# Attention outputs divided and gated as they leave PSUM, with the order of work drawn anew

## The chip, the cores and the metric

The kernel runs on one core of a Trainium2 chip. The core has five engines with instruction queues of their own: TensorE (PE in the profile; PEld is its weight load), VectorE (DVE), ScalarE (ACT), GpSimd (POOL) and SyncE (SP), which here issues all DMAs. Each queue is worked off in its order; engines wait for each other through semaphores. SBUF is the on-chip memory, PSUM the accumulator memory that TensorE writes. The metric is device time in microseconds (us) from start to end of one execution.

## The reference

Two layers are applied to x (1024 tokens x 1024 channels). Shortened, with shapes left out:

```
h = rms_norm(x, pre_norm);  proj = h @ w_in        # split into q, k, v and gates of three branches
oa = softmax(q1 k1) v - lam * softmax(q2 k2) v     # 6 differential heads, two softmaxes each
oa = rms_norm(oa, diff_subln) * (1 - lambda_init) * silu(dgate)
ob = softmax(q k) v * silu(ggate)                  # 6 grouped-query heads, 2 key heads
om = softmax(mq mk) mv * silu(mgate)               # 4 heads over 256 memory tokens
y = concat(oa, ob, om) @ w_out;  x = x + rms_norm(y, post_norm)
```

## The kernel before, in words

A planner in Python decides the order of everything. Each piece of work is a generator that asks for an engine (with an assumed duration and a priority), a buffer or a PSUM bank; an event loop (`Plan`) keeps an assumed clock and writes the instructions down in the order in which it starts them. On the chip only that order stands: the assumed durations (`ACT`, `DVE`, `LAT`, `DVE_FIX`, `SLACK`) and figures such as `DU` (spacing of score units) or `GS_ORDER` (order of heads) have no other effect.

A layer has three stretches. First come the projections: token tiles of 128 rows times column chunks of 256 (L520; 24 products to a chunk and tile, since each fp32 product is made as hi x hi + hi x lo + lo x hi). The first five chunks go ahead (`FIRST`); nine more (`REST`) are worked off beside the differential heads. What leaves PSUM is rotated (L661, L663), split, transposed (L707) and stored to DRAM; gate columns become (1 + tanh(g/2)) * g (L728, L736) and go to the scratch tensor `g_scr`.

Second, attention. There are 12 score items of the differential heads (two to a head), then 6 grouped (`g`) and 4 memory (`m`) heads in the order of `GS_ORDER`. An item has a pass for row maxima (L1071; L1283/L1284; L1338/L1339: a product of 512 columns, then a maximum on DVE, L942), a transposition of the negated maxima (L917), and units of 1024 scores per query block (L1081; L1295/L1296; L1349/L1350), each followed by exp on ACT (L898), an fp16 copy (L902, mostly ACT) and an fp16 remainder (L905, mostly POOL; L904 on DVE). Probabilities times values (PV, L531 to L533) take a bank called `pv`; V has a column of ones, so column 64 of the result is the row sum.

What happens to a PV result is what the change touches. Before, ACT copies 65 columns per query tile into an SBUF tile `o` (L994) and frees the bank. After a head's last PV, its closing steps run on whole heads of 512 columns: `fin_d` (L1161) for a differential head, `fin_g` (L1196) for the others; the gate comes by DMA into a tile `gt` (`gate_in`, L1108), the output goes to a tile `yst` and by DMA to `y_scr`.

Third, the output projection (L1448), normalisation and residual; the first tile's products fill the end of the attention.

PSUM: four single banks `ps` shared by the kinds of `KINDS` (third number 1), two double ones `pp`. In `KINDS` the second number is how many banks a kind may hold: `mx` (maxima) 4 before.

Of the kernel before, what the change touches and what calls it, by code (L numbers as in the profile page):

```python
# [22 lines left out]
P = 128  # L23
# [35 lines left out]
E_BUFS, E_MORE, O_BUFS = 4, 2, 3  # L59
# [9 lines left out]
DU = (3.0, 0.0)  # L69
# [3 lines left out]
GS_ORDER = ('g0', 'm0', 'g1', 'm1', 'g2', 'm2', 'g3', 'm3', 'g4', 'g5')  # L73
LAT = {"pe": 0.231, "act": 0.176, "dve": 0.165, "pool": 0.121, "hwdge": 0.65, "dma": 0.95}
DVE_FIX = 0.15
# [5 lines left out]
SLACK = 0.8  # L81

KINDS = {'un': (0.5, 2, 2), 'z': (1, 2, 2), 's0': (2, 2, 1), 's1': (0, 2, 1), 'st': (1, 4, 1), 'pv': (1, 1, 1), 'tr': (-1, 2, 1), 'mx': (2, 4, 1), 'zh': (3, 2, 1)}
# [204 lines left out]
def trunk(ctx, tc, t_in, t_out):  # L288
# [42 lines left out]
    def ACT(n, fn, prio=0, src="s"):  # L331
        return use("act", (0.2 if src == "s" else 0.17) + n / 1200.0, fn, prio)
# [31 lines left out]
    g_scr = dram.tile([P, 16, NT, HD], F32, name="g_scr")  # L364
# [53 lines left out]
    def vscale(vmax, gmx, w, sc, key):  # L418
# [20 lines left out]
        yield DVE(4, f, ops=4)  # L439
# [9 lines left out]
    def rstd_of(ss, n, inv, box, prio=0):  # L449
# [3 lines left out]
        def f():  # L453
            pool.tensor_scalar(out=u[:, :n], in0=ss, scalar1=inv, scalar2=EPS, op0=ALU.mult, op1=ALU.add)  # L454
            pool.tensor_tensor(out=r[:, :n], in0=u[:, :n], in1=mhalf[:, :n], op=ALU.pow)  # L455
# [83 lines left out]
    def make_layer(l):  # L539
# [185 lines left out]
        def put_gate(ps, t, c, freed):  # L725
# [156 lines left out]
        o_d, o_g, yst = {}, {}, {}  # L882

        def open_attn():
# [8 lines left out]
            R["o"] = Bag([at.tile([P, NT, 66], F32, name=f"o{i}") for i in range(O_BUFS)])  # L893
# [81 lines left out]
        def pv_part(it, u, es, evs, prev, mine):  # L975
# [7 lines left out]
            if it.new_o(u):  # L983
                yield from it.alloc_o()
# [8 lines left out]
            v = ps[:, 0:66 * n].rearrange("p (i d) -> p i d", d=66)  # L993
            yield ACT(65 * n, lambda: act.activation(it.o_dst(u), v[:, :, 0:65], AF.Copy), SV_PRIO, "p")  # L994
# [55 lines left out]
        def mk_d(m, prev):  # L1050
# [38 lines left out]
            it.new_o = lambda u: u == 1 and m % 2 == 0  # L1089

            def alloc_o():
                o_d[h] = []
                for _ in range(2):
                    o_d[h].append((yield take("o")))

            it.alloc_o = alloc_o
            it.o_dst = lambda u: o_d[h][m % 2][:, u - 1:u + 1, 0:65]
# [10 lines left out]
        def gate_in(hd):  # L1108
            c = {0: "dg0", 1: "dg0", 2: "dg0", 3: "dg0", 4: "dg1", 5: "dg1", 12: "dg1", 13: "dg1",
                 10: "gg1", 11: "gg1", 14: "gg1", 15: "gg1"}.get(hd, "gg0")  # L1110
            yield wait(gate_ev[c])
            i = yield take("gt")
            g = Q["v"].tile([P, NT, HD], F32, name="gt", bufs=2)
            yield wait(dmas([(g, g_scr[:, hd], 256)]))
            return g, i

        def y_tile(hd):
            if hd % 2 == 0:
                yst[hd // 2] = yield take("yst")
            return yst[hd // 2][:, :, hd % 2, :]  # L1120

        def y_done(hd):
            if hd % 2 == 1:
                kt = hd // 2
                c = kt * P
                t = yst.pop(kt)
# [34 lines left out]
        def fin_d(h, gate):  # L1161
            o = o_d.pop(h)
            cv = sc["d0" if h < 4 else "d1"]
            r = small.tile([P, 2, 8], F32, name="rz")
            if h in (0, 4):
                def f():
                    pool.tensor_scalar(out=cv[:, 2:3], in0=cv[:, 1:2], scalar1=2.0, scalar2=0.0,
                                       op0=ALU.mult, op1=ALU.add)
                    pool.tensor_tensor(out=cv[:, 3:4], in0=cv[:, 2:3], in1=sc["lam"], op=ALU.mult)

                yield POOL(1, f, FIN, ops=4)
            yield DVE(130, lambda: [dve.reciprocal(out=r[:, i], in_=o[i][:, :, 64]) for i in range(2)], FIN, ops=2)
            fi = yield take("ft")
            t = [Q["sd"].tile([P, NT, HD], F32, name="ft", bufs=2) for _ in range(2)]
            for i in range(2):
                yield DVE(512, lambda: dve.scalar_tensor_tensor(
                    out=t[i], in0=o[i][:, :, 0:64], scalar=cv[:, 2 + i:3 + i], in1=bc(r[:, i]),
                    op0=ALU.mult, op1=ALU.mult), FIN, port=True)
                free("o", o[i])
            yield DVE(512, lambda: dve.tensor_sub(out=t[0], in0=t[0], in1=t[1]), FIN, port=True)  # L1180
            yield ACT(512, lambda: act.activation(t[1], t[0], AF.Square), FIN)
            ss = small.tile([P, 8], F32, name="ss8")
            yield DVE(512, lambda: dve.tensor_reduce(out=ss, in_=t[1], axis=AX.X, op=ALU.add), FIN)
            box = []
            yield from rstd_of(ss, 8, 1.0 / HD, box, FIN)
            g, gi = gate
            yield DVE(512, lambda: dve.tensor_mul(out=t[0], in0=t[0], in1=g), FIN, port=True)
            free("gt", gi)
            ys = yield from y_tile(h)
            yield DVE(512, lambda: dve.tensor_tensor(out=ys, in0=t[0], in1=bc(box[0][:, :8]), op=ALU.mult), FIN,  # L1190
                      port=True)
            free("ft", fi)
            yield from y_done(h)

        def fin_g(hd, cv, gate):
            g, gi = gate  # L1196
            o = o_g.pop(hd)
# [701 lines left out]
```

## Time and profile before

| | us |
|---|---|
| runs | 1515.41, 1521.71, 1523.19 (median 1521.71) |
| the profiled execution | 1515.87 |
| its span, first to last instruction | 1514.1 |
[...]
| DVE / ACT / POOL busy | 1012.3 / 893.3 / 909.2 |

The page's busy times are unions of an engine's instructions; PE's idle time is the difference to the span. The view of stages (windows) gives the same by stretch. The view of waits says who ended an idle stretch, and the timeline the order of single instructions with the idle time before them in brackets.

### The profile page before, as it was taken

The numbers are of one execution on the slowest core, as the hardware profiler recorded it, in microseconds if no ns is written. First come the engines' busy times: TensorE is split into PE (matmuls) and PEld (weight loads), VectorE is DVE, ScalarE is ACT, GpSimd is POOL, SyncE is SP. The second block draws the span as 40 slices with busy tenths as digits, with TensorE's granted clock in tenths as the row PEclk, the third lists the DMA queues.
The fourth block names the chain that finished last, engine by engine and source line by source line (L and its number), as shares of the span: only waits on it lengthen the run. The fifth ranks groups of instructions, "written<-read, shape, count | busy, mean of one in ns | idle before, by whom it ended". The sixth has DMA issues, their size and how long they took to land.

```text
span 1514.1 us, 39223 instructions
## 1 busy us (share of the span) xinstructions
PE 1469.9 (97%) x15920; PEld 1362.8 (90%) x15920; DVE 1012.3 (67%) x1887; ACT 893.3 (59%) x1429; POOL 909.2 (60%) x653
## 2 busy tenths in 40 slices
PE   8999999999999999999999999999999999999997
PEld 7999989999999988888899989999999998788886
DVE  6738686777773897825466486776777649876233
ACT  5333747776677587663333346677667757686511
POOL 4233848889777586661132358579888757685400
PEclk9999999999999999999999999999999999999999
DMA  6544313233223644116164524223341256322232
GB/s 220 158 121 130 86 59 107 81 109 106 78 65 93 187 120 105 49 50 214 70 213 129 141 70 117 70 63 101 111 113 58 64 136 195 94 68 72 98 136 98
DMA packets 166658, 164.75 MB, mean 109 GB/s; under 512 B 14924, under 2 KB 140588, under 8 KB 166477
## 3 DMA queue, kind: packets, MB, share of 16 engines
q1 hardware_dynamic: 166477, 162.25, 36.7%
q8 instruction: 125, 2.05, 0.5%
q14 instruction: 56, 0.46, 0.1%
HBM read 111.74 MB, written 50.09 MB: 107 GB/s over the span
## 4 chain that ended last, share of the span: by engine, by line
PE 84%; DVE 5%; issue 3%; POOL 3%; DMA 2%; ACT 1%; SPq 1%; POOLq 0%; DVEq 0%; ACTq 0%
PE ps L520 35%; PE pp L1448 10%; PE pp L1081 6%; PE ps L1071 6%; PE ps L531 4%; PE ps L533 4%; PE ps L532 4%; PE ps L1283 3%; PE ps L1284 2%; PE pp L1295 2%; PE pp L1296 2%; POOL el L905 2%; PE ps L476 2%; DVE mx L942 1%; PE ps L707 1%
## 5 line engine op out<-in xcount | busy, mean ns | idle before, releaser
L905 POOL TENSOR_TENSOR el<-e,eh 128x1024 f16<-128x1024 f32 x254 | 562.6, 2229 | 167.3 <-ACT eh L902 160.1
L520 PE MATMUL ps<-wt,big 128*128 128x256 f32 x4608 | 642.1, 286 | 12.6 <-DVE sl L716 3.4
L520 PEld LDWEIGHTS ps<-wt,big 128*128 128x128 f32 x4608 | 605.0, 191 | 32.7 <-DVE sl L716 3.9
L942 DVE TENSOR_REDUCE mx<-ps 128x1 f32<-128x512 f32 (+1 forms) x608 | 404.0, 684 | 118.2 <-PE ps L1071 79.4
L898 ACT ACTIVATE e<-pp 128x1024 f32<-128x1024 f32 x304 | 309.2, 1023 | 99.9 <-PE pp L1081 53.8
L902 ACT ACTIVATE eh<-e 128x1024 f16<-128x1024 f32 x264 | 277.6, 1058 | 2.9
L531 PEld LDWEIGHTS <-eh 128*128 128x128 f16 x2144 | 194.4, 96 | 13.6 <-issue 9.0
L533 PEld LDWEIGHTS <-el 128*128 128x128 f16 x2144 | 196.1, 99 | 4.8 <-POOL el L905 4.2
L412 POOL TENSOR_TENSOR wt<-rt,wt 128x512 fp32r<-128x512 f32 x83 | 123.2, 1496 | 126.0 <-ACT wt L410 112.2
L532 PEld LDWEIGHTS <-eh 128*128 128x128 f16 x2144 | 196.2, 97 | 0.9 <-issue 0.8
L1071 PE MATMUL ps<-sdk,sdq 96*128 96x512 f32 x384 | 158.7, 413 | 0.8 <-DVE gs L736 0.8
L454 POOL TENSOR_SCALAR u<-ss 128x1 f32<-128x1 f32 (+3 forms) x95 | 24.2, 254 | 224.6 <-DVE ss L1589 96.1
L531 PE MATMUL ps<-vd,eh 128*128 128x65 f16 x1536 | 150.5, 193 | 0.0
L532 PE MATMUL ps<-vd,eh 128*128 128x64 f16 x1536 | 149.6, 194 | 0.0
L533 PE MATMUL ps<-vd,el 128*128 128x65 f16 x1536 | 149.1, 192 | 0.0
L1081 PE MATMUL pp<-sdq,sdk 98*128 98x256 f32 x768 | 124.9, 285 | 0.2 <-DMA sdq<-nl 0.2
L1081 PEld LDWEIGHTS pp<-sdq,sdk 98*128 98x128 f32 x768 | 113.1, 189 | 5.7 <-issue 0.6
L994 ACT ACTIVATE o<-ps 128x130 f32<-128x130 f32 (+1 forms) x160 | 46.1, 288 | 92.0 <-PE ps L533 91.4
L1295 PE MATMUL pp<-big 128*128 128x256 f32 x384 | 99.2, 290 | 0.0
L1296 PE MATMUL pp<-big 67*128 67x256 f32 x384 | 97.7, 286 | 1.3 <-DMA big<-nl 1.2
L410 ACT ACTIVATE wt<-rt 128x512 fp32r<-128x512 f32 x124 | 75.1, 630 | 18.8 <-DMA rt<-in_w_in 7.1
L455 POOL TENSOR_TENSOR r<-u,mhalf 128x1 f32<-128x1 f32 (+3 forms) x95 | 80.7, 850 | 7.9
(244 smaller groups left out, 2621.9 us busy)
## 6 DMA issues: line engine op xcount, KB each, us to landing
rt<-in_w_in SPq DMA_DIRECT2D x96, 128.0 KB
rt<-in_w_in SPq DMA_DIRECT2D x44, 256.0 KB
gt<-g_scr SPq DMA_DIRECT2D x32, 256.0 KB
rt<-in_w_out SPq DMA_DIRECT2D x32, 256.0 KB
sdq<-s_dqa SPq DMA_DIRECT2D x48, 128.0 KB
sdk<-s_dka SPq DMA_DIRECT2D x48, 128.0 KB
big<-s_gqa SPq DMA_DIRECT2D x24, 256.0 KB
big<-s_gqb SPq DMA_DIRECT2D x24, 256.0 KB
```

What stands on the lines that cost most here:

```text
L520: pe.matmul(ps, lhsT=x[:, kt, :], rhs=y[:, a, :], start=(kt == 0 and n == 0), stop=(kt == KT - 1 and n == 2))
L531: pe.matmul(o[:, 0:65], lhsT=eh, rhs=v[:, kt, 0:65], start=(kt == 0), stop=False, skip_group_check=True)
L532: pe.matmul(o[:, 0:64], lhsT=eh, rhs=v[:, kt, 66:130], start=False, stop=False, skip_group_check=True)
L533: pe.matmul(o[:, 0:65], lhsT=el, rhs=v[:, kt, 0:65], start=False, stop=(kt == n - 1), skip_group_check=True)
L898: yield ACT(1024, lambda: act.activation(e, ps, AF.Exp, scale=scale), 0, "p")
L902: yield either((ACT(1024, lambda: act.activation(eh, e, AF.Copy)), 0.0), (DVE(1024, lambda: dve.tensor_copy(out=eh, in_=e), 0, fast=True, ...
L905: (POOL(1024, lambda: pool.tensor_sub(out=el, in0=e, in1=eh)), 0.0))
L942: yield DVE(512, lambda: dve.tensor_reduce(out=out_ap, in_=src, axis=AX.X, op=ALU.max), MXP[0])
L1071: yield (512, lambda ps, n=n: pe.matmul(ps, lhsT=q()[0:96, i * P:(i + 1) * P], rhs=k()[0:96, n * 512:(n + 1) * 512], start=True, stop=True ...
L1081: pe.matmul(ps[:, a * 256:(a + 1) * 256], lhsT=k()[0:98, kt * P:(kt + 1) * P], rhs=q()[0:98, j * 256:(j + 1) * 256], start=True, stop=True)
L1295: pe.matmul(o, lhsT=ka()[:, ks], rhs=a()[:, qs], start=True, stop=False)
L1448: pe.matmul(z, lhsT=x[:, k, :], rhs=y, start=(k == KT_ORDER[0] and n == 0), stop=(k == KT_ORDER[-1] and n == 2))
```

## The change

- A PV result is divided by its row sum as it leaves PSUM. Even items of a differential head: a reciprocal on DVE, then ACT copies 64 columns per query tile with the reciprocal as scale. Odd items: reciprocal, times lambda, then on DVE one instruction per query tile, PSUM times reciprocal minus the even item's tile (the sign goes into the gain). One `o` tile per head is left instead of two, and `fin_d` shrinks to square, sum, power, two multiplications.
- Grouped and memory heads: reciprocal, times the scale of V, then one DVE instruction per query tile, PSUM times reciprocal times gate, written over the gate. `fin_g` is gone. The gate is loaded straight into the output tile `yst` (two heads in one DMA of 512 KB), before the first PV result of the pair may leave PSUM. `g_scr` is laid out by pairs of heads.
- The sub-norm gain is multiplied into PSUM before the gating instruction instead of after it.
- `GS_ORDER`: grouped heads go two ahead of memory heads. `KINDS`: `mx` holds 3 banks instead of 4. `DU` 3.0 to 3.17, `SLACK` 0.8 to 0.88, assumed costs of ACT and DVE changed.

```diff
-GS_ORDER = ('g0', 'm0', 'g1', 'm1', 'g2', 'm2', 'g3', 'm3', 'g4', 'g5')
+GS_ORDER = ('g0', 'g1', 'm0', 'g2', 'm1', 'g3', 'm2', 'g4', 'm3', 'g5')
-... 'mx': (2, 4, 1) ...
+... 'mx': (2, 3, 1) ...
@@ pv_part
-            yield ACT(65 * n, lambda: act.activation(it.o_dst(u), v[:, :, 0:65], AF.Copy), SV_PRIO, "p")
+            yield from it.evict(it.q0(u), ps[:, 0:66 * n].rearrange("p (i d) -> p i d", d=66), n)
@@ mk_d
+            def evict(q0, v, n):
+                r = small.tile([P, 4], F32, name="rv")
+                if m % 2 == 0:
...
+                    yield DVE(n, lambda: dve.reciprocal(out=r[:, :n], in_=v[:, :, 64]), SV_PRIO)
+                    yield ACT(HD * n, lambda: [act.activation(o[:, q0 + i, :], v[:, i, 0:HD], AF.Copy,
+                                                              scale=r[:, i:i + 1]) for i in range(n)], SV_PRIO, "p", n)
+                else:
...
+                        for i in range(n):
+                            dve.scalar_tensor_tensor(out=o[:, q0 + i, :], in0=v[:, i, 0:HD], scalar=r[:, i:i + 1],
+                                                     in1=o[:, q0 + i, :], op0=ALU.mult, op1=ALU.subtract)
@@ fin_d, the DVE part
-                yield DVE(512, lambda: dve.scalar_tensor_tensor(      # twice
-                    out=t[i], in0=o[i][:, :, 0:64], scalar=cv[:, 2 + i:3 + i], in1=bc(r[:, i]),
-            yield DVE(512, lambda: dve.tensor_sub(out=t[0], in0=t[0], in1=t[1]), FIN, port=True)
-            yield DVE(512, lambda: dve.tensor_mul(out=t[0], in0=t[0], in1=g), FIN, port=True)
-            yield DVE(512, lambda: dve.tensor_tensor(out=ys, in0=t[0], in1=bc(box[0][:, :8]), op=ALU.mult), FIN,
+            yield DVE(512, lambda: dve.tensor_tensor(out=o, in0=o, in1=bc(box[0][:, :8]), op=ALU.mult), FIN, port=True)
+            yield DVE(512, lambda: dve.tensor_mul(out=g, in0=o, in1=g), FIN, port=True)
@@ fin_g becomes gated
-            yield DVE(60, lambda: dve.reciprocal(out=r, in_=o[:, :, 64]), FIN)
-            yield DVE(512, lambda: dve.scalar_tensor_tensor(out=g, in0=g, scalar=cv()[:, 1:2], in1=bc(r),
-            yield DVE(512, lambda: dve.tensor_tensor(out=t, in0=o[:, :, 0:64], in1=g, op=ALU.mult), FIN, port=True)
+                yield wait(has)                                       # the gate has landed
+                    dve.reciprocal(out=r[:, :n], in_=v[:, :, 64])
+                    dve.tensor_scalar(out=r[:, :n], in0=r[:, :n], scalar1=cv()[:, 1:2], scalar2=None, op0=ALU.mult)
+                    for i in range(n):
+                        dve.scalar_tensor_tensor(out=g[:, q0 + i, :], in0=v[:, i, 0:HD], scalar=r[:, i:i + 1],
+                                                 in1=g[:, q0 + i, :], op0=ALU.mult, op1=ALU.mult)
```

How the order moves, at three places. First PE beside the differential heads of layer 0 (`ps_` banks; L520 is L523 after, L707 is L709, L1071 and L1081 are L1070 and L1080). Before:

```order
L1081 MATMUL pp_76<-sdq_1518,sdk_1520 128x256 x4
L520 MATMUL ps_79<-wt,big 128x256 x18
L1081 MATMUL pp_75<-sdq_1518,sdk_1520 128x256 x4
L520 MATMUL ps_79<-wt,big 128x256 x6
L707 MATMUL ps_80<-ident,nat 128x128 x2
L520 MATMUL ps_79<-wt,big 128x256 x6
```

A chunk ends in bank 79 with the fourth row (24 products) and the next chunk starts in the same bank one transposition later. The corresponding stretch after:

```order
L523 MATMUL ps_78<-wt,big 128x256 x6
L709 MATMUL ps_80<-ident,nat 128x128
L1070 MATMUL ps_77<-sdk_1524,sdq_1522 128x512
L523 MATMUL ps_78<-wt,big 128x256 x6
L1070 MATMUL ps_79<-sdk_1524,sdq_1522 128x512
L1080 MATMUL pp_75<-sdq_1523,sdk_1525 128x256 x4
```

Products for maxima and a score unit now stand between the pieces of a chunk.

Second, DVE in the stretch of grouped heads, layer 0 (`mx` are maxima, `rg`, `rv` reciprocals, `yst` the gated output). Before:

```order
L942 TENSOR_REDUCE mx<-ps_78 128x1
L1200 RECIPROCAL rg<-o_1530 128x8
L1201 SCALAR_TENSOR_TENSOR gt<-gt,vc,rg 128x512
L942 TENSOR_REDUCE mx<-ps_80 128x1
L1204 TENSOR_TENSOR yst_8471<-o_1530,gt 128x8x64
L942 TENSOR_REDUCE mx<-ps_77 128x1
```

After (the maximum is L944):

```order
L944 TENSOR_REDUCE mx<-ps_80 128x1
L1200 RECIPROCAL rv<-ps_79 128x2
L1201 TENSOR_SCALAR rv<-rv,vc 128x2
L1203 SCALAR_TENSOR_TENSOR yst_118<-ps_79,rv,yst_118 128x64 x2
L944 TENSOR_REDUCE mx<-ps_77 128x1
L944 TENSOR_REDUCE mx<-ps_78 128x1
```

Two instructions of 512 columns per head have become, for each PV result, a reciprocal, a multiplication and one instruction per query tile that reads PSUM.

Third, SP where the grouped heads begin in layer 0 (`g_scr<-gs` is the last gate of the projections going out, `gt` or `yst` the gate coming back, `big<-s_gqa` the queries of a grouped head, `rt` weights). Before:

```order
L346 DMA big<-nl 1x8x128
L346 DMA rt<-in_w_out 128x512
L346 DMA g_scr<-gs 128x4x128
L346 DMA rt<-in_w_out 128x512
L346 DMA gt<-g_scr 128x512
```

After:

```order
L346 DMA g_scr<-gs 128x2x256
L346 DMA rt<-in_w_out 128x512
L346 DMA yst_118<-g_scr 128x1024
L346 DMA big<-s_gqa_102 64x1024 x2
L346 DMA big<-s_gqa_103 64x1024
```

The gate of the first pair of heads comes back in one transfer of twice the size, and the queries of the third grouped head stand behind it.

## Rows read from the trace of the kernel before

**Rows 1.** Stages: us, busy (x count) of PE, PEld, DVE, ACT, POOL, PEclk, DMA.

```profile
120.00:520.00 400.00, 394.24 (x4723) 376.60 (x4722) 284.82 (x590) 261.51 (x413) 293.50 (x207) 1.00 0.34 97
520.00:680.00 160.00, 152.27 (x1998) 133.59 (x1997) 119.11 (x164) 118.60 (x158) 114.10 (x53) 1.00 0.32 86
...
880.00:1260.00 380.00, 373.98 (x4582) 357.83 (x4581) 268.88 (x558) 253.07 (x400) 285.55 (x202) 1.00 0.34 95
1260.00:1420.00 160.00, 152.63 (x1972) 134.16 (x1971) 118.83 (x165) 122.71 (x161) 118.14 (x54) 0.99 0.32 85
...
sum 1514.00, PE 1469.87 PEld 1362.83 DVE 1012.34 ACT 893.29 POOL 909.23; mean PE 146.99 PEld 136.28 DVE 101.23 ACT 89.33 POOL 90.92
```

**Rows 2.** Waits of PE: engine, line, for whom; total us, times, longest.

```profile
PE ps L533 <- POOL el L905: 3.6, 5, 1.1
PE ps L520 <- DVE sl L716: 3.4, 2, 1.7
...
PE ps L1339 <- DMA big<-s_gqb: 2.4, 2, 1.8
```

**Rows 3.** Timeline of PE, differential stretch: start us, us, instructions, [idle before <-releaser].

```profile
189.51 0.88 PE L520 MATMUL ps<-wt,big 128*128 128x256 f32 x6
190.23 0.38 PE L707 MATMUL ps<-ident,nat 128*128 128x128 f32 x2
192.22 0.98 PE L520 MATMUL ps<-wt,big 128*128 128x256 f32 x6 [1.61 <-DVE vg L645]
```

**Rows 4.** Timeline of DVE, differential stretch.

```profile
219.32 2.55 DVE L1176 SCALAR_TENSOR_TENSOR ft<-o,vc,rz 128x512 f32<-128x512 f32 x1
```

**Rows 5.** DVE groups by shape: xcount | busy us, mean ns | idle before.

```profile
L1204 DVE TENSOR_TENSOR yst<-o,gt 128x512 f32<-128x512 f32 x20 | 35.6, 1779 | 0.2
...
L1176 DVE SCALAR_TENSOR_TENSOR ft<-o,vc,rz 128x512 f32<-128x512 f32 x24 | 29.2, 1216 | 0.0
L1201 DVE SCALAR_TENSOR_TENSOR gt<-gt,vc,rg 128x512 f32<-128x512 f32 x20 | 28.7, 1433 | 0.5
...
L1180 DVE TENSOR_TENSOR ft<-ft 128x512 f32<-128x512 f32 x12 | 18.7, 1561 | 0.0
...
L1190 DVE TENSOR_TENSOR yst<-ft,r 128x512 f32<-128x512 f32 x12 | 15.9, 1321 | 3.1 <-POOL r L455 3.1
...
L1187 DVE TENSOR_TENSOR ft<-ft,gt 128x512 f32<-128x512 f32 x12 | 11.6, 969 | 0.0
...
L645 DVE SCALAR_TENSOR_TENSOR vg<-ps,vc,vg 128x128 f16<-128x128 f32 x16 | 5.5, 345 | 3.2 <-ACT vg L644 3.2
...
L436 DVE RECIPROCAL vc<-vc 128x1 f32<-128x1 f32 x8 | 1.3, 164 | 0.3
```

**Rows 6.** ACT and POOL groups of the page.

```profile
L905 POOL TENSOR_TENSOR el<-e,eh 128x1024 f16<-128x1024 f32 x254 | 562.6, 2229 | 167.3 <-ACT eh L902 160.1
...
L898 ACT ACTIVATE e<-pp 128x1024 f32<-128x1024 f32 x304 | 309.2, 1023 | 99.9 <-PE pp L1081 53.8
L902 ACT ACTIVATE eh<-e 128x1024 f16<-128x1024 f32 x264 | 277.6, 1058 | 2.9
...
L994 ACT ACTIVATE o<-ps 128x130 f32<-128x130 f32 (+1 forms) x160 | 46.1, 288 | 92.0 <-PE ps L533 91.4
```

**Rows 7.** ACT group by shape: a PSUM copy with a scale per partition.

```profile
L644 ACT ACTIVATE vg<-ps,vc 128x128 f16<-128x128 f32 x16 | 5.9, 370 | 15.6 <-PE ps L520 6.7 <-DVE nat L663 6.4 <-DVE wm L423 2.5
```

**Rows 8.** Line L905: duration ns min/median/max, first and last start us.

```profile
L905 POOL TENSOR_TENSOR el<-e,eh x254: 2120/2150/3137, 146.5 to 1417.8; 128x1024 f16<-128x1024 f32 x127
```

**Rows 9.** Timeline of PE, a memory head's last unit and the next one's maxima.

```profile
561.65 0.40 PE L1350 MATMUL pp<-big 67*128 67x512 f32 x1
...
568.75 0.39 PE L1339 MATMUL ps<-big 65*128 65x256 f32 x1 [1.78 <-DMA big<-s_gqb]
```

**Rows 10.** Timeline of SP, the last gate going out and its return.

```profile
512.81 0.38 SPq L346 DMA_DIRECT2D g_scr<-gs  x1
...
515.92 0.33 SPq L346 DMA_DIRECT2D gt<-g_scr  x1
```

More of the change, by code (lines that the diff above doesn't have):

```diff
@@ L1159, in bc, with fin_d @@
             return r.unsqueeze(2).broadcast_to([P, NT, HD])
-        def fin_d(h, gate):
+        def fin_d(h, g):
             o = o_d.pop(h)
-            cv = sc["d0" if h < 4 else "d1"]
-            r = small.tile([P, 2, 8], F32, name="rz")
-            if h in (0, 4):
-                def f():
[L1167 to L1175, printed above, removed]
-                yield DVE(512, lambda: dve.scalar_tensor_tensor(
-                    out=t[i], in0=o[i][:, :, 0:64], scalar=cv[:, 2 + i:3 + i], in1=bc(r[:, i]),
-                    op0=ALU.mult, op1=ALU.mult), FIN, port=True)
-                free("o", o[i])
-            yield DVE(512, lambda: dve.tensor_sub(out=t[0], in0=t[0], in1=t[1]), FIN, port=True)
[L1181 to L1186, printed above, removed]
-            yield DVE(512, lambda: dve.tensor_mul(out=t[0], in0=t[0], in1=g), FIN, port=True)
-            free("gt", gi)
-            ys = yield from y_tile(h)
-            yield DVE(512, lambda: dve.tensor_tensor(out=ys, in0=t[0], in1=bc(box[0][:, :8]), op=ALU.mult), FIN,
-                      port=True)
-            free("ft", fi)
-            yield from y_done(h)
@@ L1195, in fin_g @@
[L1195 to L1207 removed]
+            fi = yield take("ft")
@@ new lines, in fin_d @@
+            sq = Q["sd"].tile([P, NT, HD], F32, name="ft", bufs=1)
+            yield ACT(512, lambda: act.activation(sq, o, AF.Square), FIN)
+            ss = small.tile([P, 8], F32, name="ss8")
+            yield DVE(512, lambda: dve.tensor_reduce(out=ss, in_=sq, axis=AX.X, op=ALU.add), FIN)
+            free("ft", fi)
+            box = []
+            yield from rstd_of(ss, 8, 1.0 / HD, box, FIN, sc["d0" if h < 4 else "d1"][:, 3:4])
+            yield DVE(512, lambda: dve.tensor_tensor(out=o, in0=o, in1=bc(box[0][:, :8]), op=ALU.mult), FIN, port=True)
@@ new lines, in fin_d, with gated, evict, fin @@
+            yield DVE(512, lambda: dve.tensor_mul(out=g, in0=o, in1=g), FIN, port=True)
+            free("o", o)
+            yield from y_done(h)
+        def gated(it, hd, cv):
+            box, has = [], Event()
+            def evict(q0, v, n):
+                r = small.tile([P, 4], F32, name="rv")
+                yield wait(has)
+                g = box[0]
+                def f():
+                    dve.reciprocal(out=r[:, :n], in_=v[:, :, 64])
+                    dve.tensor_scalar(out=r[:, :n], in0=r[:, :n], scalar1=cv()[:, 1:2], scalar2=None, op0=ALU.mult)
+                    for i in range(n):
+                        dve.scalar_tensor_tensor(out=g[:, q0 + i, :], in0=v[:, i, 0:HD], scalar=r[:, i:i + 1],
+                                                 in1=g[:, q0 + i, :], op0=ALU.mult, op1=ALU.mult)
+                yield DVE(HD * n, f, SV_PRIO, ops=n + 2)
+            def fin():
+                box.append((yield from gate_in(hd)))
+                has.fire(pl)
+                yield wait(it.pv_done)
+                yield from y_done(hd)
+            it.evict, it.fin = evict, fin
```

130 lines of the change are left out of this document (55 added, 75 removed).

## The prediction, made before the changed kernel ran

> **What bounds the kernel now.** I read the busy times by stage first. PE is busy 1469.9 of 1514 us [rows 1], at full clock, and the change gives it the same products as before: the order has as many PE rows after as before. So the change can give back only PE's idle time, 44 us, and cost only by adding to it. Start (0 to 20 us) and tail hold what is not in the four stretches of attention; the change doesn't touch them. The four stretches are idle for 400 - 394.2 = 5.8, 160 - 152.3 = 7.7, 380 - 374.0 = 6.0 and 160 - 152.6 = 7.4 us [rows 1], in all 26.9 us: the most that could be won, 1.8%. In the stretches of differential heads (120 to 520, 880 to 1260) DVE is busy 71%; in those of grouped and memory heads (520 to 680, 1260 to 1420) DVE, ACT and POOL are all at 71 to 77% and take turns at being late.
>
> Then I read the waits of PE and went to each in the timeline. There are three sorts. (a) PE waits for a PSUM bank whose last holder is still being read by DVE or ACT: at 190.23 a chunk has just ended, the next one goes into the same bank, and PE stands 1.61 us [rows 2, 3]. (b) PE waits in the middle of a PV for the fp16 remainder from POOL, 3.6 us in five waits [rows 2]. (c) PE waits for queries that are loaded once the head before has let go of their buffer, 2.4 us in two waits of one line [rows 2].
>
> **The change part by part.** *DVE.* Gone are six kinds of 512-column instructions: 29.2 + 18.7 + 15.9 + 11.6 for the differential heads, 28.7 + 35.6 for the others, 139.7 us [rows 5]. New are 160 reciprocals against 44 before (116 x 0.164 = 19), 112 multiplications of two or four columns (priced alike, 18), 256 instructions of 64 columns that read PSUM, and 24 multiplications of 512 columns in SBUF (0.97 to 1.32 us each by the two like them, 23 to 32, I take 27) [rows 5]. The 64-column instruction is not in the trace: below is the 0.164 us of one element, above the 0.345 us of 128 columns with a pointer scalar [rows 5]; I take the middle, 0.25 us, 64 us (42 to 88). Sum 128 us (102 to 157): DVE gains 12 us (38 gained to 17 lost). That is nothing in itself, since DVE does not bound. What changes is the grain: the closing steps went as lumps of 1.2 to 1.8 us, and one took 2.55 us at 219.32 while the instruction that frees a bank stood behind it; PE then stood 1.7 us for `sl` L716 [rows 2, 4]. Lumps of that sort fall from five to two per differential head and from two to none per other head.
>
> *ACT.* 160 copies, 46.1 us, go [rows 6]; 96 copies of 64 columns with a scale come. Nearest is 0.370 us for 128 columns with a scale [rows 7]; half of that is the lower bound, all of it the upper; I take 0.3, 29 us (18 to 36). ACT gains 17 us, mostly beside grouped heads, where nothing comes back to it.
>
> *Order, differential heads.* I counted in the order how much PE work lies between the end of a chunk or transposition in a bank and the next product in that bank, with 0.12 us per 256 columns (six in 0.72 us, [rows 3]) and in proportion for others. The case in rows 3 needed 192.22 - 190.23 = 2.0 us. Below 2.0 us lie 16 places per layer before, 10.6 us short in all, the shortest at 0.14 us; after, 11 places, 5.2 us short, the shortest at 0.71 us. Measured idle was 5.8 and 6.0, or 0.56 of the count. After, 0.56 x 5.2 = 2.9 us: 3 us less per layer, 6 us in all. Bounds: none of it (the same 5.8, if DVE delays elsewhere) to all but 1 us (10 us).
>
> *Order, grouped and memory heads.* A unit needs exp 1.02, copy 1.06 and remainder at least 2.12 us (mean 2.23) before its PV, some 4.6 us with the hand-overs [rows 6, 8]. The order gave four PVs per layer less than that (3.3 to 4.3 us), 3.8 us short; now one, 2.2 us short, behind the first memory head. That is 1.6 us less per layer. Against it, loads. From the end of a memory head's last unit (561.65 + 0.40) to the product that had the queries (568.75) went 6.7 us [rows 9]. PE work between the two was 4.3, 4.0 and 5.1 us for the three memory heads that follow another one, and is now 3.2, 5.1 and 5.9; this is even, and the first coincides with the short PV. New is the third grouped head: 12.5 us before, 3.1 now. And the first grouped pair's gate is now needed before the first PV result may leave its bank, of which there is one for PVs. The round trip is long: going out to coming back took 3.1 us at 512.81 [rows 10], and the load back has 512 KB. Its landing is not in the trace. The order puts some 9 us of DVE work between the last gating instruction and the one that waits; that covers a landing within about 5 us, and otherwise DVE stands with the maxima queued behind it, and PE with the second PV. I price both together at 1.5 us per layer (0 to 4). Where the DVE lumps fall away I take 0.5 us per layer. So 1.6 + 0.5 - 1.5 = 0.6 per layer, 1 us in all, between +8 lost and -8 gained.
>
> *The rest.* `mx` with 3 banks is in the count of banks. Spacing 3.17 instead of 3.0 moves score units later and chunks earlier; PE has chunks to fill with until the stretch ends in both. The last head's chain before the last transpositions (reciprocal, 1.43, 1.78 us, [rows 5]) becomes about 0.8 us, but the order has taken away the products that covered it: zero.
>
> **Sum.** -6 -1 = -7 us. On the profiled execution, 1515.87 us (span 1514.1 and 1.8 around it), that is 1509. The runs shown are two-fold: this one and 1515.41 on one side, 1521.71 and 1523.19 on the other. The middle is 1519, the median of the three runs 2.7 above that. I forecast from the middle: 1512 us.
>
> **Rivals.** *Given back at the start of the grouped heads* (about 0, 1515 to 1521). The gate comes late and the third head's queries too: 3.1 us of work against 6.7 us needed is 3.6 us, 7 us over two layers, and the 7 are gone. For it: the waits for queries in the trace are of just this kind [rows 2, 9]. Against: part of it coincides with waits that were there.
>
> *More than counted* (1499 to 1508). DVE instructions with two SBUF operands and POOL hold each other up: the multiplication by the gate took 1.78 us mean where a like one took 0.97 [rows 5], and the remainder on POOL has a mean of 2.23 us against a floor of 2.12 [rows 6, 8]. 254 remainders x 0.1 = 25 us of POOL, and the 35.6 + 28.7 us of DVE lumps are gone where both are late. If that frees the grouped stretches of two thirds of their 15 us, the time is 1519 - 6 - 10 = 1503. Against: the waits seen there are for queries and for units just issued, which a shorter remainder only shortens by 0.1.
>
> [...]
>
> *Slower: DVE at the head of the line* (about 1528). Before, ACT stood waiting for PVs, 91.4 us over 160 copies, 0.57 each [rows 6]. Now DVE does, with maxima behind it in its queue and only three banks for them. Beside grouped heads DVE has 160 - 119 = 41 us free per layer [rows 1] and 32 such results. It decides from 41 / 32 = 1.3 us each; at 1.4 us, with the dependent small instructions 0.05 us slower than taken, the stretch grows by some 5 us per layer, 10 in all. Against: the results come when the order expects them, and 0.57 is less than half of 1.3.
>
> **How the numbers follow.** Forecast (gain of 2 to 13 us, 1506 to 1517) 0.53; given back 0.18; more 0.13; slower 0.16. A measurement of this kernel tells 0.5%, 7.6 us, from no change: below 1511.4 or above 1526.6. Of the forecast 0.27 lies below 1511.4 and 0.26 above, all of "more" below; of the slower case 0.03 stays within. Faster 0.40, same 0.47, slower 0.13. For 8 in 10 I reach to 1500 and to 1526; the forecast's own range is 1506 to 1517.
>
> **What would show it.** Right: PE idle in 120 to 520 and 880 to 1260 falls from 5.8 and 6.0 to about 3; waits of PE for the readers of a bank (L716, L645 and their like) at most half of before; the 64-column instruction at 0.2 to 0.3 us; waits for the remainder under 2 us; a wait of 1 to 3 us for `big` or behind the first `yst` load where grouped heads begin. Wrong: idle in the differential stretches still above 5 us (then bank distance was not what held PE), idle in the grouped stretches above 10 (gate, queries) or under 4 (POOL), DVE waiting for PV more than 1.3 us each.

## The result: 2.4% slower, and the profile after

The changed kernel took 1556.5 us (median of 4 runs, 1554.7 to 1558.3) against 1520.0 us: ratio 1.0238 (95% interval 1.0208 to 1.0268). The forecast was 1512, with 1526 as the upper end. The profiled execution took 1557.7 us with a span of 1555.8, 41.7 more than the span of before. PE is busy 1486.7 us: 24.9 us of the difference are idle time of PE (69.1 against 44.2) and 16.8 are busy time, although the products are the same; the granted clock is 0.987 against 0.997 (TensorE is at half its full clock, 0.50, for 39.0 us of this span, against 8.0 before; at 0.50 a product of 256 columns (L523) starts 0.213 us after the one before it, at 1.00 0.120 us, medians).

The stages after, to set beside [rows 1] (the columns are the same):

```profile
120.00:520.00 400.00, 392.65 (x4710) 373.72 (x4708) 306.31 (x680) 261.67 (x410) 283.35 (x198) 1.00 0.32 93
520.00:680.00 160.00, 142.27 (x1810) 123.39 (x1809) 131.41 (x269) 104.73 (x120) 105.72 (x53) 0.98 0.31 87
880.00:1260.00 380.00, 373.45 (x4506) 356.03 (x4505) 288.12 (x646) 251.02 (x397) 270.26 (x191) 1.00 0.31 91
1260.00:1420.00 160.00, 143.75 (x1639) 124.51 (x1638) 135.96 (x265) 90.04 (x107) 93.87 (x48) 0.94 0.39 109
```

Read the grouped stretches (second and fourth row): PE's idle time went from 7.7 and 7.4 us to 17.7 and 16.2, and DVE does 12 and 17 us more there. The clock is lower there too, 0.98 and 0.94 against 1.00 and 0.99. Since stages shift against fixed windows, I also took the times at which the first and the last product of the grouped maxima (L1283 before, L1290 after) start. From the start to the first one it is 2.5 us *less* than before; the grouped stretch of layer 0 is 15.0 us longer, the way to layer 1's grouped heads 5.3, their stretch 19.7, the rest 4.2. So 35 of the 41.7 us are lost in the two grouped stretches.

The waits of PE after (those of before are [rows 2]):

```profile
PE ps L534 <- DVE yst L1203: 10.6, 9, 1.9
PE ps L1290 <- DVE yst L1203: 6.7, 6, 2.4
PE ps L1070 <- DVE o L1107: 4.7, 4, 1.3
PE ps L919 <- DVE yst L1203: 4.6, 2, 2.6
PE ps L709 <- DVE nat L665: 3.5, 1, 3.5
```

Four of the five name the new evictions. L1203 and L1107 are the last instructions of an eviction, not the slow ones. DVE's groups by shape show which is (busy us, mean ns, idle before; `rv` is the reciprocal):

```profile
L1201 DVE TENSOR_SCALAR rv<-rv,vc 128x2 f32<-128x2 f32 x48 | 54.0, 1125 | 1.7
L1203 DVE SCALAR_TENSOR_TENSOR yst<-ps,rv,yst 128x64 f32<-128x64 f32 x160 | 36.6, 278 | 2.3
L1105 DVE TENSOR_SCALAR rv<-rv,lam 128x2 f32<-128x2 f32 x48 | 35.7, 744 | 1.7
L1107 DVE SCALAR_TENSOR_TENSOR o<-ps,rv,o 128x64 f32<-128x64 f32 x96 | 22.8, 279 | 1.7
L1201 DVE TENSOR_SCALAR rv<-rv,vc 128x4 f32<-128x4 f32 x16 | 14.2, 888 | 0.6
L1104 DVE RECIPROCAL rv<-ps 128x2 f32<-128x2 f32 x48 | 8.1, 168 | 41.5 <-PE ps L536 41.5
L1200 DVE RECIPROCAL rv<-ps 128x2 f32<-128x2 f32 x48 | 8.0, 166 | 40.9 <-PE ps L536 40.9
```

The multiplication of the reciprocal by lambda (L1105) or by V's scale (L1201), two or four columns, takes 104 us in 112 instructions. Its shortest takes 0.23 us, its longest 2.2. The eviction's other pieces cost about what was forecast: 0.28 us for the 64 columns on DVE (0.25), 0.17 for a reciprocal (0.164), and on ACT 0.31 for each of the 96 copies (0.3; [rows 7]), which overlap in part and keep it busy for 24.7 us in all. One case in the timeline (start, us, instruction, [idle before <- releaser]):

```profile
559.25 2.44 POOL L907 TENSOR_TENSOR el<-e,eh 128x1024 f16<-128x1024 f32 x1
559.63 0.16 DVE L1200 RECIPROCAL rv<-ps 128x2 f32<-128x2 f32 x1
559.83 1.89 DVE L1201 TENSOR_SCALAR rv<-rv,vc 128x2 f32<-128x2 f32 x1
...
561.75 0.48 DVE L1203 SCALAR_TENSOR_TENSOR yst<-ps,rv,yst 128x64 f32<-128x64 f32 x2
...
562.28 0.51 PE L1290 MATMUL ps<-big 128*128 128x512 f32 x1 [2.42 <-DVE yst L1203]
```

POOL's remainder ends at 561.69, the multiplication, begun at 559.83, at 561.72, and PE waits 2.42 us for the bank behind it. Of the 112, 67 take over 0.4 us, together 78 us beyond 0.23 us each, and each of the 67 ends within 0.03 us of the end of a POOL instruction (61 remainders, and six of L412, POOL's part in splitting weights). Ten more begin inside a POOL instruction and take 0.23 us all the same: six in the last 0.16 us of a remainder, and four beside a power of two or four columns (L458, 0.69 to 1.01 us). So not every POOL instruction holds the multiplication up. None of the 256 instructions of 64 columns (one input in PSUM) takes over 0.4 us, though 108 of them begin while POOL is at work.

At the layer boundary stands a second, smaller thing: the redrawn order has put the scaling of the sub-norm's gain ahead in DVE's queue, before its transfer has landed. DVE waits 4.14 us for it, where it did not wait before, and PE 3.55 us behind DVE.

```profile
788.34 0.20 DVE L620 TENSOR_SCALAR sub<-sub 128x64 f32<-128x64 f32 x1 [4.14 <-DMA sub<-in_diff_subln]
...
791.04 0.47 PE L709 MATMUL ps<-ident,nat 128*128 128x128 f32 x1 [3.55 <-DVE nat L665]
```

### The profile page after: what moved, and what is told of

It reads as the page before. It is cut to its first block, busy times and chain, and to the rows that moved or that the text cites. A ratio compares the mean times of both kernels' runs of the same rounds, so it can differ in the third digit from the quotient of the medians.

```text
span 1555.8 us, 39490 instructions
## 1 busy us (share of the span) xinstructions
PE 1486.7 (96%) x15920; PEld 1371.1 (88%) x15920; DVE 1099.4 (71%) x2314; ACT 880.4 (57%) x1363; POOL 890.0 (57%) x644
## 4 chain that ended last, share of the span: by engine, by line
PE 81%; DVE 13%; DMA 3%; issue 2%; ACT 1%; SPq 0%; POOL 0%; POOLq 0%; DVEq 0%; ACTq 0%
PE ps L523 34%; PE pp L1436 9%; PE ps L1070 6%; PE pp L1080 5%; PE ps L534 4%; PE ps L535 4%; PE ps L536 4%; DVE mx L944 3%; DVE rv L1201 3%; PE ps L1290 2%; PE pp L1302 2%; PE pp L1303 2%; PE ps L1291 2%; PE ps L479 2%; PE ps L709 1%
## 5 line engine op out<-in xcount | busy, mean ns | idle before, releaser
L907 POOL TENSOR_TENSOR el<-e,eh 128x1024 f16<-128x1024 f32 x252 | 549.4, 2193 | 210.4 <-ACT eh L904 131.0
L523 PE MATMUL ps<-wt,big 128*128 128x256 f32 x4608 | 642.1, 286 | 2.0 <-DVE nat L665 0.7
L523 PEld LDWEIGHTS ps<-wt,big 128*128 128x128 f32 x4608 | 605.2, 191 | 21.2 <-DVE mx L944 3.1
L944 DVE TENSOR_REDUCE mx<-ps 128x1 f32<-128x512 f32 (+1 forms) x608 | 404.8, 684 | 72.4 <-PE ps L1070 43.9
L904 ACT ACTIVATE eh<-e 128x1024 f16<-128x1024 f32 x260 | 272.4, 1059 | 7.4 <-PE ps L536 4.2
L412 POOL TENSOR_TENSOR wt<-rt,wt 128x512 fp32r<-128x512 f32 x80 | 113.1, 1425 | 116.9 <-ACT wt L410 87.4
L1070 PE MATMUL ps<-sdk,sdq 96*128 96x512 f32 x384 | 158.4, 412 | 5.0 <-DVE o L1107 4.7
L457 POOL TENSOR_SCALAR u<-ss 128x1 f32<-128x1 f32 (+2 forms) x83 | 18.2, 219 | 189.0 <-DVE ss L1577 93.1
L1080 PE MATMUL pp<-sdq,sdk 98*128 98x256 f32 x768 | 123.9, 283 | 0.0
L1080 PEld LDWEIGHTS pp<-sdq,sdk 98*128 98x128 f32 x768 | 113.2, 190 | 5.8
L907 POOL TENSOR_TENSOR elm<-e,ehm 128x1024 f16<-128x1024 f32 x34 | 76.0, 2243 | 35.9 <-ACT ehm L904 33.7
L410 ACT ACTIVATE wt<-rt 128x512 fp32r<-128x512 f32 x124 | 76.0, 629 | 32.8 <-DMA rt<-in_w_out 13.8
L1290 PE MATMUL ps<-big 128*128 128x512 f32 x192 | 83.5, 435 | 10.2 <-DVE yst L1203 6.7
```

Of the source, the lines that this page charges most:

```text
L523: pe.matmul(ps, lhsT=x[:, kt, :], rhs=y[:, a, :], start=(kt == 0 and n == 0), stop=(kt == KT - 1 and n == 2))
L904: yield either((ACT(1024, lambda: act.activation(eh, e, AF.Copy)), 0.0), (DVE(1024, lambda: dve.tensor_copy(out=eh, in_=e), 0, fast=True, ...
L907: (POOL(1024, lambda: pool.tensor_sub(out=el, in0=e, in1=eh)), 0.0))
L944: yield DVE(512, lambda: dve.tensor_reduce(out=out_ap, in_=src, axis=AX.X, op=ALU.max), MXP[0])
L1070: yield (512, lambda ps, n=n: pe.matmul(ps, lhsT=q()[0:96, i * P:(i + 1) * P], rhs=k()[0:96, n * 512:(n + 1) * 512], start=True, stop=True ...
L1080: pe.matmul(ps[:, a * 256:(a + 1) * 256], lhsT=k()[0:98, kt * P:(kt + 1) * P], rhs=q()[0:98, j * 256:(j + 1) * 256], start=True, stop=True)
```

## The experiments

Theory A: the multiplication, SBUF to SBUF, waits for POOL's remainder. B: the redrawn order is the cause. C: DVE has too much on the path of a PV, whatever each piece costs. Ratios are against the kernel before, with 95% intervals. In the diffs, r and v64 stand for `r[:, :n]` and `v[:, :, 64]`.

**e1: multiply out of PSUM, then divide.** Same order of instructions.

```diff
-  dve.reciprocal(out=r, in_=v64)
-  dve.tensor_scalar(out=r, in0=r, scalar1=sc["lam"], ..., op0=ALU.mult)
+  dve.tensor_scalar(out=r, in0=v64, scalar1=sc["ilam"], ..., op0=ALU.mult)   # 1 / lambda; likewise 2 * V's scale
+  dve.reciprocal(out=r, in_=r)
```

> As the changed kernel, in the same order of instructions, but the 112 small multiplications read their 2 or 4 columns out of PSUM (times 1/lambda, or twice the reciprocal of V's scale) and the reciprocal comes after them in SBUF. Theory A (the multiplication that reads SBUF and writes SBUF waits for GpSimd's remainder of 2.2 us, and the PV bank and TensorE wait behind it): its mean falls from 0.74 to 1.13 us to about 0.25 us, the waits of TensorE for yst (10.6 + 6.7 + 4.6 + 2.0 us) mostly go, the clock comes back in the grouped stretches, and the time is 1515 to 1530. Theory B (the redrawn order and figures are the cause, the multiplication is hidden): within 8 us of the changed kernel, 1548 to 1560. Theory C (VectorE does too much at the head of the PV path, whatever each piece costs): 1540 to 1556, with the waits of TensorE for yst still there.

1526.6 us, ratio 1.0039 (1.0025 to 1.0052), as A said. The same groups of DVE:

```profile
L1106 DVE TENSOR_SCALAR rv<-ps,ilam 128x2 f32<-128x2 f32 x48 | 10.4, 217 | 41.8 <-PE ps L536 41.8
L1202 DVE TENSOR_SCALAR rv<-ps,vc 128x2 f32<-128x2 f32 x48 | 10.4, 217 | 58.9 <-PE ps L536 58.9
...
L1203 DVE RECIPROCAL rv<-rv 128x2 f32<-128x2 f32 x48 | 8.0, 166 | 1.6
L1107 DVE RECIPROCAL rv<-rv 128x2 f32<-128x2 f32 x48 | 8.0, 166 | 1.6
```

The 112 multiplications take 24.3 us instead of 104; 30 of the 36 us lost are back. Now the reciprocal is the small instruction from SBUF to SBUF: 77 of the 112 begin inside a POOL instruction, and none takes over 0.18 us. So what waits isn't everything that stays in SBUF.

**e2: no multiplication.** The two lines are deleted, so the output lacks lambda and V's scale.

> As the changed kernel without the 112 small multiplications: the output lacks lambda in the differential heads and V's scale in the others. Theory A: 1512 to 1528, a little under the kernel that scales in PSUM (112 x 0.25 us less VectorE work, some of it beside other work). Theory B: 1545 to 1558. Theory C: in between, about 1540, since 112 of 368 instructions on that path go.

1519.8, ratio 0.9989 (0.9976 to 1.0001), as A said. With the multiplication free the changed kernel only equals the one before, so the gain that was forecast is missing even then.

**e3 and e4: the halves of the change.** e3 has the old eviction and gate with the new figures (`GS_ORDER`, `KINDS`, `DU`, `SLACK`, assumed costs), e4 the new eviction with the old figures.

> The kernel before (its eviction, its gate) with the redrawn figures of the plan alone: grouped heads two ahead, three products for maxima, the new estimates of ACT and VectorE. Theory A: no slower than the kernel before by more than 0.5%, 1508 to 1528. Theory B: most of the loss, 1540 to 1556. Theory C: as A.

> The changed eviction and gate with the plan's figures and the order of heads of the kernel before. Theory A: still slow, 1540 to 1565, VectorE's small multiplication at 0.7 us or more in the mean, TensorE waiting for yst. Theory B: near the kernel before, 1515 to 1528. Theory C: as A.

e3: 1539.6, ratio 1.0125 (1.0095 to 1.0155). Neither A (at most 1528) nor B (1540 to 1556) had that; A lacks 12 us (it says nothing of a redrawn plan). e4: 1562.0, ratio 1.0272 (1.0251 to 1.0294), as A said. The figures cost the old eviction 18 us, and putting them back makes the new one slower still: a set of figures is good for the code it was chosen for.

**e5 and e6: the multiplication twice**, the first into a tile that nobody reads; e5 in SBUF, e6 out of PSUM.

```diff
   dve.reciprocal(out=r, in_=v64)
+  dve.tensor_scalar(out=r2, in0=r, scalar1=sc["lam"], ..., op0=ALU.mult)     # e5; e6: e1's out of PSUM, doubled
   dve.tensor_scalar(out=r, in0=r, scalar1=sc["lam"], ..., op0=ALU.mult)
```

> The changed kernel with each of the 112 multiplications that read and write SBUF run twice, the first of the two into a tile that nobody reads. Theory A, if each such instruction has to wait for a free moment of GpSimd: both means 0.6 us or more and 1575 to 1600. Theory A in a milder form, where the second of the pair finds the way open because the first has just waited for it: the second at 0.23 to 0.4 us and 1560 to 1572. Theory C (VectorE has too much on this path, whatever it is): 112 x 0.23 = 26 us more VectorE work for both kernels with a doubled multiplication, so this one and the PSUM one lose alike, 6 to 12 us.

> The kernel that multiplies first, out of PSUM (1526.6), with each of the 112 multiplications run twice, the first into a tile that nobody reads. Theory A: the second costs its own 0.17 to 0.25 us on VectorE and is mostly hidden, 1526 to 1533. Theory C: 1535 or more.

e5: 1613.9, ratio 1.0594 (1.0543 to 1.0645), 57 us over the changed kernel and more than the 1575 to 1600 of A's stricter form. e6: 1523.1, ratio 1.0017 (1.0000 to 1.0034), no slower than e1. The same number of instructions was added to both, so C falls.

```profile
L1204 DVE TENSOR_SCALAR rv<-rv,vc 128x2 f32<-128x2 f32 x48 | 51.9, 1082 | 1.7
L1205 DVE TENSOR_SCALAR rv<-rv,vc 128x2 f32<-128x2 f32 x48 | 42.5, 885 | 1.7
L1106 DVE TENSOR_SCALAR rv<-rv,lam 128x2 f32<-128x2 f32 x48 | 32.7, 681 | 1.7
L1107 DVE TENSOR_SCALAR rv<-rv,lam 128x2 f32<-128x2 f32 x48 | 22.6, 472 | 1.7
```

L1205 stands right behind L1204, which has often just waited, and in 20 of its 64 cases it takes over 0.4 us again, each ending with a POOL instruction. In differential heads this is rarer (L1107, 6 of 48).

**e7 and e8: old figures on e1.** e7 puts back `GS_ORDER`, e8 all figures.

> The kernel that multiplies first, out of PSUM, with one figure put back: grouped and memory heads in turn, as in the kernel before. With the multiplication cheap, TensorE idles no longer than before (43 us against 44), but its granted clock is below 1.00 at the start of the grouped heads (0.91, 0.83, 0.91 from 520 us on; 0.83, 0.98, 0.84 from 1280 us on), where it was 1.00 before. Theory D (grouped heads two ahead start the stage with VectorE waits and lose the clock there): the clock is back and the time 1512 to 1520. Theory E (the lost clock comes with the eviction, by the maxima behind the PV bank, whatever the order): 1522 to 1530.

> The kernel that multiplies first, out of PSUM, with all the plan's figures put back (order of heads, products that may wait, the estimates of VectorE and ACT). Theory D: 1512 to 1520. Theory E: 1522 to 1532, as the changed kernel itself got 5 us slower with the old figures.

1541.4 (ratio 1.0122, 1.0090 to 1.0154) and 1540.9 (1.0125, 1.0090 to 1.0161): D falls clearly, and both are slower than E said. Since putting figures back draws the whole plan anew, this does not show what two grouped heads ahead cost in e1's own plan.

**e9: two inputs.** The multiplication as a `tensor_tensor`, still in SBUF.

```diff
-  dve.tensor_scalar(out=r, in0=r, scalar1=sc["lam"], ..., op0=ALU.mult)
+  dve.tensor_tensor(out=r, in0=r, in1=sc["lam"].broadcast_to([P, n]), op=ALU.mult)
```

> The changed kernel with its 112 small SBUF multiplications in another form: a tensor_tensor of the reciprocal with lambda, or V's constant, spread along the columns, so still SBUF to SBUF but with two inputs. Theory A1 (what waits for GpSimd is the tensor_scalar form; the reciprocals from SBUF to SBUF beside the same remainders took 179 ns at most): no multiplication over 0.4 us, and about the time of the kernel that multiplies out of PSUM, 1520 to 1532. Theory A2 (any small multiplication with all its operands in SBUF waits): still 0.7 us or more in the mean, 1548 to 1562.

1557.1, ratio 1.0239 (1.0193 to 1.0285): A1 falls.

```profile
L1201 DVE TENSOR_TENSOR rv<-rv,vc 128x2 f32<-128x2 f32 x48 | 50.9, 1060 | 1.6
L1105 DVE TENSOR_TENSOR rv<-rv,lam 128x2 f32<-128x2 f32 x48 | 25.0, 521 | 1.6
```

64 of the 112 take over 0.4 us, all begun inside a POOL instruction; the shortest takes 0.16, the longest 3.6, through two remainders. So this `tensor_scalar` with its input in SBUF waited (67 of the changed kernel's 112 over 0.4 us), and this `tensor_tensor` with both inputs there waited; the reciprocal didn't (0.18 us at most in e1), and neither did e1's multiplications out of PSUM (0.22 at most) nor the changed kernel's instructions of 64 columns with one input in PSUM (0.29 at most). Why these forms differ is not shown. Two more things stay open: the four multiplications beside L458 that did not wait, and waits through more than one POOL instruction (here, and in e13).

**e10 and e11: the plan of e1.** e10 delays the gain's scaling by 4.5 us in the planner's clock (L620 of the boundary); e11 tells the planner that an eviction is 0.09 us dearer.

```diff
             yield wait(dmas(lst, 1))
+            yield "until", pl.t + 4.5                 # e10
...
-                yield DVE(HD * n, f, SV_PRIO, ops=n + 2)
+                yield DVE(HD * n, f, SV_PRIO, ops=n + 2.6)    # e11, both places
```

> The kernel that multiplies first, out of PSUM, with the scaling of the sub-norm's gain (one VectorE instruction per layer) planned 4.5 us later after its transfer is asked for. At the layer boundary VectorE stood 4.1 us at the head of its queue for that transfer, and TensorE waited 2.7 us. Theory F (this is part of what is left): the wait for nat at L709 goes and the time falls by 2 to 6 us, to 1518 to 1525. Rival: the plan is drawn anew by that one delay and something else is late, 1524 to 1540.

> The kernel that multiplies first, out of PSUM, with the planner told that an eviction on VectorE costs 0.09 us more (0.83 us for two columns of heads, as its trace shows, for 0.74). Theory G (the plan is too tight since it counts the eviction too cheap): 1512 to 1522, with fewer waits of TensorE for VectorE in the grouped stretches. Rival: the plan is drawn anew and the time moves either way, 1520 to 1545, as it did with the order of heads.

1533.1 (ratio 1.0080, 1.0049 to 1.0111) and 1541.2 (1.0136, 1.0104 to 1.0168): both came out as their rivals said. In e10 the two waits at the boundary are gone, but these lead its list, where e1 has 3.3 us for POOL's remainder and none for `nl`:

```profile
PE ps L536 <- POOL el L910: 6.2, 7, 1.8
PE pp L1306 <- DMA big<-nl: 4.4, 2, 2.4
```

**e12: the same wait, plan kept.** On e1; the planner still books the time, but no instruction is written.

```diff
-  yield DVE(64, lambda: dve.tensor_scalar(out=Q["sub1"], in0=Q["sub1"], scalar1=-0.5 * (1.0 - lam0), ...))
+  yield DVE(64, lambda: None)
-  dve.tensor_tensor(out=v, in0=v, in1=<sub1 spread over heads>, op=ALU.mult)
+  dve.scalar_tensor_tensor(out=v, in0=v, scalar=-0.5 * (1.0 - lam0), in1=<the same>, op0=ALU.mult, op1=ALU.mult)
```

> The kernel that multiplies first, out of PSUM, in the same plan, without the instruction on VectorE that scales the sub-norm's gain (its factor goes into the multiplication of the gate in PSUM, as a scalar_tensor_tensor in place of a tensor_tensor). Theory F (the wait of VectorE for that gain at the layer boundary is part of what is left): the 4.1 us wait of VectorE and the 2.7 us wait of TensorE at L709 go, 1519 to 1525. Rival (another late transfer or the clock takes it back): 1525 to 1529.

1518.9, ratio 0.9985 (0.9967 to 1.0004), just past the gaining end of what F gave. No wait for the gain is left, and from 760 to 800 us PE is busy throughout (37.26 us of 40 in e1). The time fell by 7.7 us against e1, and that wait of PE was 2.7. In the two profiled executions TensorE is at half clock (0.50) for 22.2 us instead of 43.7, which can make up the rest; that removing the wait is the reason for it is not shown.

**e13 and e14: shorter remainders.** Each of POOL's remainders as two instructions of 512 columns; e13 on the changed kernel, e14 on e12.

```diff
-  POOL(1024, lambda: pool.tensor_sub(out=el, in0=e, in1=eh))
+  POOL(1024, lambda: [pool.tensor_sub(out=el[:, k:k + 512], in0=e[:, k:k + 512], in1=eh[:, k:k + 512]) for k in (0, 512)])
```

> The changed kernel in its own plan, its SBUF multiplications as they are, with each of GpSimd's remainders of 1024 columns (2.2 us) cut into two instructions of 512. Theory A (the multiplication waits until the GpSimd instruction under way ends): the longest falls from 2.2 to about 1.1 to 1.3 us, the mean of the 112 from 0.93 to 0.5 to 0.6 us, and the time from 1556 to 1533 to 1545. Rival (it waits for something else that goes on beside the remainder, or the remainders follow each other too closely to let it in): as long as before, 1552 to 1562, or more for the dearer remainders.

> The kernel of e12 with GpSimd's remainders cut in two as in e13. Other VectorE instructions with both inputs in SBUF wait for the remainders too; with shorter ones these waits shrink. Theory A: 2 to 6 us under e12, if the 252 further instructions cost GpSimd no more than 0.1 us each beside other work; rival: GpSimd's remainder is late more often (TensorE waited 3.3 us for it in e1) and the time is 1 to 6 us above e12.

e13: 1539.2, ratio 1.0102 (1.0073 to 1.0132): 17 us back by touching POOL alone, a time within A's 1533 to 1545. DVE's groups and POOL's:

```profile
L907 POOL TENSOR_TENSOR el<-e,eh 128x512 f16<-128x512 f32 x504 | 599.5, 1218 | 169.1 <-ACT eh L904 57.4
...
L1202 DVE TENSOR_SCALAR rv<-rv,vc 128x2 f32<-128x2 f32 x48 | 30.6, 636 | 1.7
L1106 DVE TENSOR_SCALAR rv<-rv,lam 128x2 f32<-128x2 f32 x48 | 25.1, 522 | 1.7
L1202 DVE TENSOR_SCALAR rv<-rv,vc 128x4 f32<-128x4 f32 x16 | 14.7, 916 | 0.6
```

The 112 take 70 us instead of 104, 0.63 in the mean (A: 0.5 to 0.6), and 111 of them at most 1.27 (A: 1.1 to 1.3). The last one took 6.6 us, through six of POOL's instructions that follow each other without a gap:

```profile
602.61 3.40 POOL L907 TENSOR_TENSOR el<-e,eh 128x512 f16<-128x512 f32 x3
603.86 6.62 DVE L1202 TENSOR_SCALAR rv<-rv,vc 128x4 f32<-128x4 f32 x1
605.98 4.48 POOL L907 TENSOR_TENSOR elm<-e,ehm 128x512 f16<-128x512 f32 x4
```

So it doesn't always get in at the first end of a POOL instruction; A had not foreseen that, and what decides it stays open. e14: 1519.7, ratio 0.9987 (0.9969 to 1.0004), the same as e12; neither its gain nor its loss can be measured. That bears on e13: DVE's other work got shorter there too (60 us less in all, 34 of them the multiplications). In e14, where the multiplications read PSUM, DVE is busy 24 us less than in e12 and no time comes back, so e13's 17 us are most likely those of the multiplications.

## Why the prediction was wrong

**The step that failed** is in the sum for DVE: "112 multiplications of two or four columns (priced alike, 18)". They took 104 us, 0.93 each. The price, 0.164 us, came from a reciprocal of one column [rows 5], another operation; reciprocals did not wait for POOL in e1 (0.18 us at most). The prediction also gave DVE's sum no weight ("nothing in itself, since DVE does not bound"), but these 112 stand between a PV result and the release of its bank, and PE waited behind them. The trace of before held the warning: DVE's steps of 512 columns with both inputs in SBUF had means far apart for like work, 1779 against 969 ns [rows 5], and the prediction used this only for the rival on the gaining side. DVE's sum thus came to 87 us more instead of 12 less. With the multiplication out of PSUM (e1) it is 8 us more, within the bounds given.

**Slower, as a rival,** had the place right (a PV result waits for DVE, maxima queue behind it, the bank is held) and the mechanism wrong. It was to decide from 1.3 us of waiting of DVE for each PV. DVE waited 41.5 us for the 48 results of odd items in differential heads and 47.0 for the 64 in the others, 0.9 and 0.7 us each. It was not idle at the head of its line but stuck inside an instruction. The rival allowed the small instructions 0.05 us more than taken; the multiplication took 0.76 more.

**Differential heads, 6 us:** the step was right, and the changed kernel hid it. Its idle time there, 7.3 and 6.5 us, would by the prediction's own test have refuted the count of bank distances. e1 has the same order, with a cheap multiplication:

```profile
120.00:520.00 400.00, 396.79 (x4720) 378.84 (x4718) 294.53 (x681) 263.15 (x413) 284.60 (x198) 0.99 0.33 94
520.00:680.00 160.00, 150.06 (x1925) 133.00 (x1925) 109.06 (x276) 108.66 (x122) 111.99 (x55) 0.96 0.32 85
880.00:1260.00 380.00, 376.81 (x4587) 359.89 (x4587) 279.02 (x660) 251.42 (x396) 273.59 (x192) 1.00 0.32 90
1260.00:1420.00 160.00, 152.74 (x1882) 135.45 (x1881) 117.00 (x278) 112.52 (x129) 112.24 (x55) 0.96 0.36 98
```

PE is idle 3.2 us in each of the first and third rows; the forecast was 2.9. The waits that the count was about have gone too: before, PE waited 1.7, 1.6 and 1.5 us in each of these two stretches for L716, L645 and L715 to read a chunk's bank, in e1 0.2 (L647); at the place of L715's, near 147 us and its like in layer 1, it now waits 1.5 us for L665. The way to the grouped heads is 2.9 us shorter in layer 0 and 2.0 in layer 1.

**Grouped and memory heads, 1 us gained:** wrong in sign also without the multiplication. The distance from the first to the last product of the grouped maxima was 156.2 and 157.3 us before, and is 165.3 and 162.3 in e1, 159.3 and 162.4 in e12. PE's idle time there is 2.2 us more than before in layer 0 and as before in layer 1 (9.9 and 7.3 us in e1). The rest is the clock: in e1 TensorE is at half clock for 13.6 us in either stretch, before for none and 3.4, and at half the clock that costs up to 6.8 and 5.1 us more than before (an estimate). One term is found: behind the first eviction with a gate, PE waited 1.8 us per layer (3.7 us in all, at e1's line of the transposed maxima). That is the first rival's place, but not its load: in both layers DVE had a remainder of 1.7 us in hand, and DVE's list of waits names no load of `yst`. What else the order costs there was not separated.

**The clock** was priced nowhere. In e1 PE is idle 43.2 us, 1.0 less than before, and yet busy 13.8 us more: the whole difference of the spans (12.8) comes from stretches at the lower clock, 43.7 us against 8.0 (an estimate: with 0.213 us in place of 0.120 for a product, the 35.7 us more at half clock cost some 15.6). It isn't the order alone. e1 and e12 have the same order, but for the scaling of the gain, and the same stall of PE, 1.51 us, between 146 and 148 us, in rows of 2 us (PEclk is the third number from the end); e1:

```profile
146.00:148.00 2.00, 0.49 (x6) 0.31 (x4) 1.93 (x9) 1.55 (x2) 1.75 (x4) 1.00 0.00 0
148.00:150.00 2.00, 1.91 (x11) 1.71 (x10) 2.00 (x6) 1.82 (x3) 1.92 (x5) 0.65 0.00 0
150.00:152.00 2.00, 2.00 (x9) 1.76 (x9) 1.20 (x8) 0.79 (x1) 2.00 (x2) 0.50 0.03 8
```

and e12:

```profile
146.00:148.00 2.00, 0.59 (x5) 0.57 (x5) 1.93 (x8) 1.97 (x2) 1.67 (x5) 1.00 0.00 0
148.00:150.00 2.00, 1.91 (x14) 1.60 (x13) 1.97 (x7) 1.83 (x3) 2.00 (x4) 1.00 0.00 0
150.00:152.00 2.00, 2.00 (x18) 1.96 (x17) 1.93 (x7) 0.69 (x2) 2.00 (x2) 1.00 0.04 8
```

After the stall e1's clock drops to half (0.50), e12's stays full (1.00). The changed kernel's, with 1.54 us idle there, stays full too (1.00 in all three rows). So a profile of one execution says less about a few us than its rows suggest, and why the clock falls in one and not in the other stays open.

**The redrawn order** was taken as neutral beyond the counted places. e3, e7, e8, e10 and e11 each drew a plan anew, e10 by no more than 4.5 us at one instruction. e3 came out 18 us above the kernel before, the others 15, 14, 7 and 15 above e1. The prediction also held that the change leaves alone what lies outside the four stretches of attention; the wait at the layer boundary (PE 3.5 us, 2.7 in e1) is there. Only changes that left the plan as it was (e1, e2, e5, e6, e9, e12, e13, e14) show what an edit itself is worth.

## What to carry to other kernels

Price a small instruction from a row of the same operation, with its operands in the same memory and the same neighbour at work; without such a row, take for its upper bound at least the longest instruction of the engine that it may have to wait for, not the shortest row. (Here a wait once went through six of them, 6.6 us.) If a scalar must be applied to something that comes out of PSUM, apply it in an instruction that reads PSUM, before the result lies in SBUF (here 0.22 us in the mean in place of 0.93). When a planner draws the order, change an instruction with the plan held fixed before believing what the edit costs.

## What was not expected of the hardware

- Two columns cost about as much here as a step of 512 (0.97 to 1.78 us in the mean [rows 5]): a `tensor_scalar` of 128x2 in SBUF took 0.23 us alone and up to 2.2 us beside POOL's remainder, 0.74 to 1.13 in the mean; with its input in PSUM it took 0.20 to 0.22 in all 112 cases of e1.
- A reciprocal from SBUF to SBUF, of two or four columns, never waited (0.165 to 0.179 us, 77 of 112 begun inside a POOL instruction).
- Cutting POOL's instructions in two (2.19 us to 2 x 1.22) cost POOL 47 us more work, and was worth 17 us.
